# The order of 24 gate tiles beside two block inverses: sigmoid tiles first, silu tiles last

## The chip, the cores and the metric

The program runs on one core of a Trainium2 chip. The metric is the time of one launch on the device in microseconds (us). The engines of the core run side by side, each through its own instructions in order: PE (TensorE, matmuls), DVE (VectorE), ACT (ScalarE), POOL (GpSimd) and SP (SyncE, which here only issues DMAs; ACT issues some too).

## The reference

One layer of a diffusion backbone: 2048 latent and 256 context tokens of width 1024, float32. The normalized input `h` goes through one wide projection that feeds two token mixers and four gates; the mixers' outputs are gated and merged:

```python
qkv, beta_r, decay_r, kb, vb = _split_cols(h @ w_state, STATE_SIZES)
za, qb, zb, ga, gb = _split_cols(h @ w_rest, REST_SIZES)       # 512, 512, 512, 1024, 1024 columns
qa, ka, va, g, bt = _gdn_inputs(qkv, beta_r, decay_r, conv_w, a_log, dt_bias)
oa, _, _ = _gdn_bidir(qa, ka, va, g, bt, s_f, s_b, True)       # mixer A, a scan over 64-token chunks
ya = _rmsnorm(oa, gdn_norm_w) * silu(za)
ob = _latent_attention(qb, kb, vb, kb_c, vb_c, sink)           # mixer B, windowed attention
yb = ob * silu(zb)
y = sigmoid(ga) * (ya @ w_proj_a) + sigmoid(gb) * (yb @ w_proj_b)
x = x + gate[:, None] * (y @ w_out)
```

Mixer A is a gated delta rule in chunked form. Per chunk and head it needs the inverse of a unit lower triangular 64x64 matrix (`triangular_solve` in the reference). `gate` is a third of `silu(c) @ w_mod + b_mod`.

## The kernel before, in words

**Stages.** The input projection for q, k, v; then the gates of token blocks 2 and 3 beside two batches of block inverses (about 629 to 910 us of the profiled execution, the stretch that the change edits); then the scan of mixer A, beside which the gates of token blocks 1 and 0 run as fill; attention; the rest of the gates; projections and output.

**A gate tile.** The gates' 3072 columns are cut in 24 feature tiles of 128, numbered `m`: 0 to 3 are `za`, 4 to 7 `zb` (both under silu), 8 to 15 `ga`, 16 to 23 `gb` (both under sigmoid). Tokens are cut in four blocks of 512 (`gi`). `gates(ms, gis, ...)` goes through the tiles in the order of the list `ms`, and for each through the token blocks of `gis`; it asks for the next tile's weights after the first block of a tile (`rest`, L804; `gates`, L830). `beside` is another piece of work, here the gate third of `w_mod` (`mod_gate`, L212), of which one bit is written down per tile.

**Weights.** float32 products are made of three matmuls of halves. `weights` (L235) loads a tile in two pieces (`wr`, L241, on SP's queue, two buffers), rounds each to its high half `wh` (L243 on ACT in this stretch, L245 on POOL for other callers), and has DVE subtract to get the low half `wl` (L246). `wh` and `wl` have two buffers each. `fm_dense` (L521) multiplies: for each of 8 slices of 128 rows one matmul wh x hh (L524), one wh x hl (L525), one wl x hh (L526): 24 matmuls, 128x128 by 128x512, into one of three PSUM buffers (`rps`).

**What follows the matmuls** is in `rest_run` (L811): ACT takes tanh of half the sum out of PSUM into `rt` (L816, two buffers). For a silu tile DVE then reads PSUM again and makes (tanh + 1) * sum (L818). A store sends `rt` to DRAM (L819): silu tiles on SP's queue, sigmoid tiles on ACT's:

```python
        S.activation(t, ps, AF.Tanh, scale=0.5)
        if m < 8:
            V.scalar_tensor_tensor(t, t, 1.0, ps, op0=ALU.add, op1=ALU.mult)
        (dma if m < 8 else adma)(dst[gi][mm], t)
```

**The inverses.** `base` (L720) inverts 128 matrices at a time, one per partition, and is called twice. It loads `nb` and `N` (L733, L734, on SP's queue, up to 1 MB each), scales the rows of the lower and the upper half by `nb` (L737, L739, four instructions each), then makes 62 steps of a multiply (L747) and an add (L749), both on DVE, 62 to 992 elements wide; POOL clears the upper triangles (L754), a store sends the result to `Xsp` (L759). `base4` (L764) does the four remaining chunks during the scan (L784 and on).

**mod_gate** loads `w_mod` rows (L220, SP's queue), scales them on ACT (L221), adds them up on POOL (L223), sums over partitions with one matmul (L227), adds the bias on DVE (L230, L231) and stores.

**The scan** loads its operands on SP's queue (L1002, L1004, L1083, L1085 and others), merges inverses of 64 tokens to 128 (L1011 to L1034: TensorE `mtp`, `myp`, `mep`; DVE L1019, L1025) and then goes through a chain per step: `ksps` (L1093), DVE L1095, `vps` (L1099), DVE L1102, `sps` (L1111), the state S on DVE (L1114 at first, L1117 later). The memory of its first loads is that of the blocks `hh` and `hl` of the gates before, so these loads wait for the last matmul of the first gates.

**What sets the order.** A list scheduler puts the instructions of the whole program on each engine in an order of its own when the program is built; what is written in the kernel gives the dependences and a rank. On the chip that order is fixed: an engine runs its instructions one by one, and one that waits holds up all behind it.

Of the kernel before, what the change touches and what calls it, by code (L numbers as in the profile page):

```python
# [32 lines left out]
def hybrid(tc, ins, out, dbg=None, upto=9):  # L33
    nc = tc.nc
    V, S, G, T = nc.vector, nc.scalar, nc.gpsimd, nc.tensor
    ctx = ExitStack()
    with ctx:
        _hybrid(ctx, tc, nc, V, S, G, T, ins, out, dbg, upto)


def _hybrid(ctx, tc, nc, V, S, G, T, ins, out, dbg, upto):
# [103 lines left out]
    def psum(tag, shape, dt=F32, name=None):  # L145
        _, p, banks = pst["left" if tag in pst["left"][2] else "right"]
        return p.tile(shape, dt, name=name or tag, tag=tag, bufs=banks[tag])
# [64 lines left out]
    def mod_gate(pool, ones):  # L212


        for n in range(2):
            cs_ = slice(2 * D + n * 512, 2 * D + n * 512 + 512)
            gacc = pool.tile([128, 512], F32, name="gacc", bufs=1)
            for k in range(KT):
                wm = pool.tile([128, 512], F32, name="wmg", bufs=2)
                dma(wm, ins["w_mod"][0, k * 128:(k + 1) * 128, cs_])  # L220
                S.activation(wm if k else gacc, wm, AF.Copy, scale=silc[:, k, 0:1])  # L221
                if k:
                    G.tensor_tensor(gacc, gacc, wm, op=ALU.add)  # L223
                yield
            yield
            gsum = psum(f"gd{n}", [1, 512], name=f"gsum{n}")
            T.matmul(gsum, lhsT=ones[:, 0:1], rhs=gacc, start=True, stop=True)  # L227
            grow = ev.tile([1, 512], F32, name="grow", tag="rt")
            dma(grow, ins["b_mod"][:, cs_])
            V.tensor_tensor(grow, gsum, grow, op=ALU.add)  # L230
            V.tensor_scalar(grow, grow, 0.5, None, op0=ALU.mult)  # L231
            dma(gsp[:, n * 512:n * 512 + 512], grow)
            yield
# [274 lines left out]
    le, ge, gt, lt, ones = (mats[:, j] for j in range(5))  # L508
# [295 lines left out]
    def rest(ev, m, by_act):  # L804

        col, dst, mm = ((C_ZA, zasp, m) if m < 4 else (C_ZB, zbsp, m - 4) if m < 8 else
                        (C_GA, gasp, m - 8) if m < 16 else (C_GB, gbsp, m - 16))
        w = weights(w_in[:, col + mm * 128:col + mm * 128 + 128], KT, by_act)
        return w, dst, mm

    def rest_run(ev, job, m, gi):  # L811
        w, dst, mm = job
        ps = acc([128, 512], name="rps")
        fm_dense(ps, w, hh[gi], hl[gi])
        t = ev.tile([128, 512], F32, name="rt", bufs=2)
# [4 lines that stand above are left out]
# [10 lines left out]
    def gates(ms, gis, beside=(), by_act=False):  # L830
        beside = iter(beside)
        job = rest(ev, ms[0], by_act)
        for i, m in enumerate(ms):
            for j, gi in enumerate(gis):
                rest_run(ev, job, m, gi)
                if j == 0:
                    nxt = rest(ev, ms[i + 1], by_act) if i + 1 < len(ms) else None
                    next(beside, None)
            job = nxt
# [1 line left out]
    bs2_ = tc.tile_pool(name="base2", bufs=1, reuse_waits="tile")  # L841
    bs2 = bs2_.__enter__()
    with tc.tile_pool(name="gate", bufs=1, reuse_waits="tile") as gp:
        gates(list(range(24)), (2, 3), mod_gate(gp, ones), by_act=True)
    LAST = (LAT(14, 15), LAT(0, 1))
    for si, (fr, bk, np_) in enumerate((([0, 1] + LAT(*range(0, 6)), [0, 1] + LAT(*range(10, 16)), bs),
                                        (LAT(*range(6, 14)), LAT(*range(2, 10)), bs2))):
# [532 lines left out]
```

## Time and profile before

| | |
|---|---|
| time, median of 3 runs | 2011.59 us (2009.54 to 2018.15) |
| the profiled execution | 2010.84 us, span 2009.1 us |
| mean granted TensorE clock | 0.988 |
| busy: PE, DVE, ACT, POOL | 96%, 70%, 39%, 33% of the span |
| busiest groups of TensorE | rps L524, L525, L526: 308.4, 306.4, 308.3 us |
| L818, DVE | 32 instructions, 664 to 690 ns each; 16 of them in the gates of blocks 2 and 3 |
| L246, DVE (all tiles) | 120 instructions of 128x512, 776 ns in the mean |

The profile is of one execution. Its times start with the first instruction of the span; an instruction is named by its line in the kernel, with what it writes and reads (`rt<-rt,rps`). An idle time is written in brackets behind the instruction that ended it, with what released that instruction. Matmuls overlap, so their listed 0.39 us is longer than the 0.23 us from one to the next; a few per cent of the matmuls are missing in the record.

### The profile page before, as it was taken

The page shows a single profiled execution, that of the slowest core. Times are in us where ns is not written, and L with a number is a line of the kernel's source. Part 1 is how long each engine was busy: PE and PEld are TensorE (multiplying, and loading weights), DVE is VectorE, ACT ScalarE, POOL GpSimd, SP SyncE. Part 2 cuts the span into 40 slices and gives each one's busy share as a digit, 9 for nine tenths or more (in the row PEclk, how much of TensorE's full clock was granted, in tenths as well). Part 3 has the DMA queues.
Part 4 walks back from the last instruction along what each step waited for, and adds up shares of the span by engine and source line. Part 5 has one row for each costly group of instructions (what it writes and reads, how often), then busy time and mean ns, then how long its engine had stood idle before and what let it go on. Part 6 is the DMA issues. An engine that isn't in the chain of part 4 may idle for free. (4 is left out here: it accounts for less than half of the span.)

```text
span 2009.1 us, 32070 instructions
## 1 busy us (share of the span) xinstructions
PE 1936.4 (96%) x11043; PEld 1625.3 (81%) x11043; DVE 1407.5 (70%) x2780; ACT 786.1 (39%) x1975; POOL 654.0 (33%) x751
## 2 busy tenths in 40 slices
PE   6999999989999999999999999999999999999999
PEld 3888888778998778877888888888778887878887
DVE  7979766667776899999777776536687878643322
ACT  5755545544443322211222233225665656531100
POOL 1752111225443212004222234323555444432221
PEclk8999999999999999999999999999999999999999
DMA  7552326764546633537887777674455555365542
GB/s 260 166 137 83 102 87 157 184 162 147 167 142 164 184 115 110 142 100 215 230 245 221 235 207 217 195 218 129 150 184 166 184 162 178 90 195 181 183 141 94
DMA packets 375511, 333.11 MB, mean 166 GB/s; under 512 B 83833, under 2 KB 299185, under 8 KB 374709
## 3 DMA queue, kind: packets, MB, share of 16 engines
q1 hardware_dynamic: 347924, 288.59, 49.7%
q10 hardware_dynamic: 27424, 42.48, 5.9%
q8 instruction: 87, 1.43, 0.3%
q14 instruction: 76, 0.61, 0.1%
HBM read 220.28 MB, written 109.13 MB: 164 GB/s over the span
## 5 line engine op out<-in xcount | busy, mean ns | idle before, releaser
L524 PE MATMUL rps<-hh,wh 128*128 128x512 f32 x768 | 308.4, 402 | 5.4 <-DVE rt L818 4.2
L526 PE MATMUL rps<-hh,wl 128*128 128x512 f32 x768 | 308.3, 402 | 0.0
L525 PE MATMUL rps<-hl,wh 128*128 128x512 f32 x768 | 306.4, 399 | 0.0
L563 DVE SCALAR_TENSOR_TENSOR cacc<-y,cw,cacc 128x512 f32<-128x512 f32 (+1 forms) x224 | 162.8, 748 | 22.4 <-ACT cacc L561 18.2
L524 PEld LDWEIGHTS rps<-hh,wh 128*128 128x128 f32 x768 | 145.0, 189 | 40.1 <-DVE rt L818 4.8
L524 PE MATMUL lps<-hh,wh 128*128 128x512 f32 (+1 forms) x448 | 171.4, 383 | 0.2 <-ACT y L634 0.2
L526 PE MATMUL lps<-hh,wl 128*128 128x512 f32 (+1 forms) x448 | 171.5, 383 | 0.0
L526 PEld LDWEIGHTS rps<-hh,wl 128*128 128x128 f32 x768 | 145.0, 189 | 32.6
L525 PE MATMUL lps<-hl,wh 128*128 128x512 f32 (+1 forms) x448 | 171.2, 382 | 0.0
L525 PEld LDWEIGHTS rps<-hl,wh 128*128 128x128 f32 x768 | 145.0, 189 | 32.4
L945 DVE TENSOR_TENSOR pl<-pt,ph 128x512 fp32r<-128x512 f32 x156 | 105.5, 686 | 42.1 <-ACT ph L943 41.2
L943 ACT CAST ph<-pt 128x512 fp32r<-128x512 f32 x156 | 90.1, 584 | 110.2 <-PE pt L941 77.2
L917 DVE CUSTOM_DVE_ANT_0 pr<-sc,band,sk 128x640 f32<-128x640 f32 (+1 forms) x128 | 106.8, 862 | 32.7 <-PE sc L913 16.9
L816 ACT ACTIVATE rt<-rps 128x512 f32<-128x512 f32 x96 | 57.2, 595 | 176.0 <-PE rps L526 159.1
L749 DVE TENSOR_TENSOR N<-N,btmp 128x62 f32<-128x62 f32 (+30 forms) x124 | 117.7, 949 | 3.0
L747 DVE TENSOR_TENSOR btmp<-N 128x62 f32<-128x62 f32 (+30 forms) x124 | 116.1, 936 | 3.1
L927 POOL TENSOR_SCALAR pr<-pr,sm 128x640 f32<-128x640 f32 (+1 forms) x128 | 99.2, 794 | 56.1 <-DVE sm L925 38.3
L1229 PE MATMUL pps<-yh,wph 128*128 128x512 f32 x256 | 105.2, 415 | 7.2 <-ACT yh L1211 5.0
L919 ACT ACTIVATE pr<-pr,sm 128x640 f32<-128x640 f32 (+1 forms) x128 | 104.0, 815 | 19.8 <-DVE sm L917 19.8
L246 DVE TENSOR_TENSOR wl<-wr,wh 128x512 fp32r<-128x512 f32 x120 | 91.6, 776 | 23.9 <-POOL wh L245 21.3
L245 POOL TENSOR_SCALAR wh<-wr 128x512 fp32r<-128x512 f32 x72 | 48.1, 683 | 167.1 <-PE lps L525 67.6
L1230 PE MATMUL pps<-yl,wph 128*128 128x512 f32 x256 | 101.7, 397 | 0.0
(301 smaller groups left out, 4922.8 us busy)
## 6 DMA issues: line engine op xcount, KB each, us to landing
wr<-in_w_in_dram SPq DMA_DIRECT2D x120, 256.0 KB
kw<-Ksp SPq DMA_DIRECT2D x28, 384.0 KB
x<-vsp SPq DMA_DIRECT2D x36, 256.0 KB
k<-ksp SPq DMA_DIRECT2D x34, 256.0 KB
kT<-kTsp SPq DMA_DIRECT2D x34, 256.0 KB
wm<-in_w_mod_dram SPq DMA_DIRECT2D x16, 512.0 KB
xt<-in_x_dram SPq DMA_DIRECT2D x16, 512.0 KB
dtl<-Dsp SPq DMA_DIRECT2D x32, 256.0 KB
```

Source lines behind the costliest of these rows:

```text
L524: T.matmul(ps, lhsT=wh[:, k], rhs=xh[:, k], start=k == 0, stop=False)
L525: T.matmul(ps, lhsT=wh[:, k], rhs=xl[:, k], start=False, stop=False)
L526: T.matmul(ps, lhsT=wl[:, k], rhs=xh[:, k], start=False, stop=k == kt - 1)
L563: V.scalar_tensor_tensor(a, y[:, t:t + n], cw[:, m, t:t + 1], a, op0=ALU.mult, op1=ALU.add)
L747: V.tensor_tensor(tv, A[:, m + 1:, m].unsqueeze(2).to_broadcast([h1 + n, r, m]), A[:, m, 0:m].unsqueeze(1).to_broadcast([h1 + n, r, m]), o ...
L749: V.tensor_tensor(A[:, m + 1:, 0:m], A[:, m + 1:, 0:m], tv, op=ALU.add)
L917: V.tensor_tensor_reduce(s_, ps[:, o:768], band[:, b0:b0 + W + 256], -0.125, sk[:, 1, hd:hd + 1], ALU.add, ALU.min, sm[:, h, 1:2])
L919: S.activation(s_, s_, AF.Exp, scale=-1.0, bias=sm[:, h, 1:2], accum_out=sm[:, h, 2:3])
L927: G.tensor_scalar(p[:, h, :W + 256], p[:, h, :W + 256], sm[:, h, 3:4], 1.0, op0=ALU.mult, op1=ALU.mult)
L945: V.tensor_tensor(pl, pt, f32(ph), op=ALU.subtract)
L1229: T.matmul(ps, lhsT=wh[:, k, ms], rhs=hs[k], start=k == 0, stop=False)
L1230: T.matmul(ps, lhsT=wh[:, k, ms], rhs=ls[k], start=False, stop=False)
```

## The change

The list of tiles of the first `gates` call is written in another order. Nothing else is edited; the later calls (`gates` at L1176, L1180 and L1251) keep theirs.

```diff
@@ -841,7 +841,7 @@
     bs2 = bs2_.__enter__()
     with tc.tile_pool(name="gate", bufs=1, reuse_waits="tile") as gp:
-        gates(list(range(24)), (2, 3), mod_gate(gp, ones), by_act=True)
+        gates(list(range(8, 24)) + list(range(8)), (2, 3), mod_gate(gp, ones), by_act=True)
     LAST = (LAT(14, 15), LAT(0, 1))
```

Since the scheduler decides, the order of the other engines' work changes too. On DVE, where the first inverse begins (L737 and L739 are its scalings, L747 its first step; - is before, + after):

```order
 L737 TENSOR_TENSOR N<-N,nb 64x1024
-L246 TENSOR_TENSOR wl<-wr,wh 128x512 x2
-L818 SCALAR_TENSOR_TENSOR rt<-rt,rps 128x512
+L246 TENSOR_TENSOR wl<-wr,wh 128x512
 L739 TENSOR_TENSOR N<-N,nb 64x16x16
 L739 TENSOR_TENSOR N<-N,nb 64x16x32
 L739 TENSOR_TENSOR N<-N,nb 64x16x48
 L739 TENSOR_TENSOR N<-N,nb 64x1024
-L818 SCALAR_TENSOR_TENSOR rt<-rt,rps 128x512
 L747 TENSOR_TENSOR btmp<-N 128x62
 L749 TENSOR_TENSOR N<-N,btmp 128x62
```

The L818 that stood before and behind the scalings of L739 are gone, and the two L246 of a tile stand apart.

On DVE in the second inverse, at the two L246 of the thirteenth tile of the list. Before:

```order
L749 TENSOR_TENSOR N<-N,btmp 128x25x38
L246 TENSOR_TENSOR wl<-wr,wh 128x512
L747 TENSOR_TENSOR btmp<-N 128x936
L246 TENSOR_TENSOR wl<-wr,wh 128x512
L749 TENSOR_TENSOR N<-N,btmp 128x24x39
```

After:

```order
L749 TENSOR_TENSOR N<-N,btmp 128x23x40
L747 TENSOR_TENSOR btmp<-N 128x902
L749 TENSOR_TENSOR N<-N,btmp 128x22x41
L246 TENSOR_TENSOR wl<-wr,wh 128x512
L747 TENSOR_TENSOR btmp<-N 128x882
L246 TENSOR_TENSOR wl<-wr,wh 128x512
L749 TENSOR_TENSOR N<-N,btmp 128x21x42
```

The pair stands four widths later: counted from the second inverse's L739, 66 instructions of L747 and L749 stand ahead of it before, and 70 after, and twelve L818 before and none after.

On SP, where the scan's first loads (L1004, L1083) begin; wr are weights. Before:

```order
L241 DMA wr<-in_w_in_dram 128x4x128 x8
L229 DMA grow<-in_b_mod_dram 1x512
L232 DMA gsp<-grow 1x512
L241 DMA wr<-in_w_in_dram 128x4x128 x8
L1004 DMA moff_10009<-offsp_91 64x256
L1004 DMA moff_10015<-offsp_92 64x256
L1083 DMA k_10055<-ksp 128x512
```

After:

```order
L819 DMA zbsp_124<-rt 128x512
L819 DMA zbsp_123<-rt 128x512
L241 DMA wr<-in_w_in_dram 128x4x128
L819 DMA zbsp_124<-rt 128x512
L241 DMA wr<-in_w_in_dram 128x4x128
L819 DMA zbsp_123<-rt 128x512
L1004 DMA moff_10009<-offsp_91 64x256
L1004 DMA moff_10015<-offsp_92 64x256
L1083 DMA k_10055<-ksp 128x512
```

The last silu stores (L819) now stand between the weight loads, and one stands straight ahead of the scan's first load. The very last one comes about 24 loads later. The 16 stores of sigmoid tiles that are first in the list are issued by ACT, each behind its tanh.

## Rows read from the trace of the kernel before

**Rows 1.** The page, part 1: busy time, share of the span, instructions.
```profile
PE   6999999989999999999999999999999999999999
```

**Rows 2.** Waits of TensorE, 600 to 1350: us in total, times, longest.
```profile
PE rps L524 <- DVE rt L818: 4.2, 1, 4.2
...
PE ksps L1093 <- DVE S L1117: 2.9, 1, 2.9
...
PE mep L1028 <- DVE moff L1025: 1.8, 1, 1.8
```

**Rows 3.** A window: each engine's busy us, granted clock (PEclk), DMA share, GB/s.
```profile
672.00:680.00 8.00, 4.35 (x10) 3.47 (x11) 7.93 (x11) 4.53 (x7) 4.22 (x4) 0.63 0.49 146
```

**Rows 4.** Timeline, TensorE: start, us, instruction, [idle before, and for what].
```profile
671.06 0.39 PE L526 MATMUL rps<-hh,wl 128*128 128x512 f32 x1
...
675.65 0.79 PE L524 MATMUL rps<-hh,wh 128*128 128x512 f32 x1 [4.20 <-DVE rt L818]
...
683.73 0.40 PE L524 MATMUL rps<-hh,wh 128*128 128x512 f32 x1
...
689.33 0.40 PE L524 MATMUL rps<-hh,wh 128*128 128x512 f32 x1
...
694.93 0.40 PE L524 MATMUL rps<-hh,wh 128*128 128x512 f32 x1
```

**Rows 5.** Timeline, VectorE, 671 to 677.
```profile
671.84 3.04 DVE L739 TENSOR_TENSOR N<-N,nb 64x256 f32<-64x256 f32 x4 [2.34 <-DMA N<-Nsp]
...
674.91 0.69 DVE L818 SCALAR_TENSOR_TENSOR rt<-rt,rps 128x512 f32<-128x512 f32 x1
...
675.51 0.87 DVE L747 TENSOR_TENSOR btmp<-N 128x342 f32<-128x342 f32 x1
...
676.42 1.47 DVE L749 TENSOR_TENSOR N<-N,btmp 128x342 f32<-128x342 f32 x1
```

**Rows 6.** Timeline, SyncE's queue and Scalar, 659 to 675.
```profile
659.94 0.33 SPq L819 DMA_DIRECT2D zasp<-rt  x1
...
662.63 0.59 ACT L816 ACTIVATE rt<-rps 128x512 f32<-128x512 f32 x1
...
672.14 0.60 ACT L816 ACTIVATE rt<-rps 128x512 f32<-128x512 f32 x1 [8.92 <-DMA zasp<-rt]
...
674.21 1.30 ACT L243 CAST wh<-wr 128x512 fp32r<-128x512 f32 x2
```

**Rows 7.** Timeline, VectorE: low halves of the weights of places 5 and 12.
```profile
691.40 0.69 DVE L246 TENSOR_TENSOR wl<-wr,wh 128x512 fp32r<-128x512 f32 x1
...
772.18 0.68 DVE L246 TENSOR_TENSOR wl<-wr,wh 128x512 fp32r<-128x512 f32 x1
```

**Rows 8.** VectorE's timeline, and POOL's groups in 744 to 772 (busy us, mean ns).
```profile
747.62 2.17 DVE L749 TENSOR_TENSOR N<-N,btmp 128x992 f32<-128x992 f32 x1
...
751.53 1.17 DVE L749 TENSOR_TENSOR N<-N,btmp 128x990 f32<-128x990 f32 x1
...
L223 POOL TENSOR_TENSOR gacc<-gacc,wmg 128x512 f32<-128x512 f32 x7 | 14.1, 2010 | 12.3 <-ACT wmg L221 9.7 <-ACT gacc L221 2.5
```

**Rows 9.** VectorE: a window, and the group of L246 in 690 to 919.
```profile
810.00:919.00 109.00, 109.00 (x466) 86.78 (x465) 102.31 (x127) 18.75 (x33) 9.91 (x12) 1.00 0.44 123
...
L246 DVE TENSOR_TENSOR wl<-wr,wh 128x512 fp32r<-128x512 f32 x42 | 30.1, 730 | 3.9 <-ACT wh L243 2.0 <-POOL wh L245 1.9
```

**Rows 10.** Timelines at the scan's start: SyncE's queue, VectorE, TensorE.
```profile
910.22 1.12 SPq L1004 DMA_DIRECT2D moff<-offsp  x2
...
938.38 0.68 DVE L1102 TENSOR_TENSOR v<-vps,brs 128x512 f32<-128x512 f32 x1
...
939.12 1.16 PE L1111 MATMUL sps<-v,k 128*128 128x128 f32 x8 [1.29 <-DVE v L1102]
```

**Rows 11.** A window of the scan, columns as in rows 3.
```profile
1262.00:1270.00 8.00, 5.11 (x35) 4.45 (x34) 6.31 (x15) 1.98 (x9) 5.66 (x8) 1.00 0.81 243
```

## The prediction

> **What bounds the kernel now.** I read the page's busy shares first. TensorE is busy for 96% of the span [rows 1], so nothing that only relieves VectorE or a queue changes the end; what counts is where TensorE waits or runs slowly. The list of TensorE's waits is therefore the second view, cut to 600 to 1350 us, the stretch whose instructions the change moves. It has one large wait in the gate stage, 4.2 us for the step L818 of VectorE, and two in the scan, 2.9 and 1.8 us [rows 2]. The third view is the clock by windows: in 672 to 680 us TensorE was granted 0.63 of full speed, so it spent most of that window at the lower of its levels (1.2 and not 2.4 GHz), right behind that wait [rows 3]. The fourth is TensorE's timeline. I call the 24 matmuls of one feature tile on one block of tokens a pass (passes 0 to 47), and a tile's position in the list its place (places 0 to 23, two passes each). Pass 6 issues its last matmul at 671.06 and, at 0.23 us a matmul, is through at 671.29. Pass 7 starts at 675.65, pass 8 at 683.73, pass 9 at 689.33, pass 10 at 694.93 [rows 4]. So the wait is 675.65 - 671.29 = 4.36 us; pass 7 lasts 8.08 where pass 8 or 9 lasts 5.60, another 2.48. One event costs 6.84 us.
>
> Why does it wait? A pass needs one of three PSUM buffers, and pass 7 gets that of pass 4. Pass 4 is a silu tile, and its buffer is read last by L818 at 674.91 on VectorE, in order behind the L739 multiplies of the second inverse, which began at 671.84 after 2.34 us of waiting for N to land [rows 5]. Scalar has its own delay: its tanh of pass 4 starts only at 672.14, after 8.92 us of waiting for the store of pass 2, issued on SyncE at 659.94 [rows 6]; that store was late because its L818 too had stood behind an L739 waiting for N. The two inverses' loads thus reach TensorE only through L818.
>
> **The change part by part.** It adds and removes no arithmetic. Sixteen L818 leave the passes 0 to 15 and return in passes 32 to 47; sixteen stores leave SyncE's queue where N, the weights and w_mod are loaded, and their data goes on Scalar's queue; the same number comes back to SyncE late.
>
> *The wait at 671 goes.* Place 2 is then a sigmoid tile, whose tanh is the last reader of PSUM. The store of pass 2 is issued by Scalar itself right behind its tanh, near 650 instead of 659.94. Even if it takes as long to land as before (659.94 to 672.14, 12.2 us) it is there at 662.4. The tanh of pass 3 ran at 662.63 [rows 6], that of pass 4 can follow at 663.3, eight us before TensorE asks at 671.29. Pass 5's buffer is asked for at 676.9. Its tanh stands behind the same w_mod scalings and casts that ended with the cast at 674.21 (1.30 us) [rows 6], so it ends by 676.1. I take the whole 6.84 as removed: 0 to 6.84.
>
> *What is late next: the low halves of the weights.* VectorE computes them (wl, L246) between the steps of the inverses, and TensorE, 6.84 us earlier, asks for them earlier. VectorE cannot start the second inverse earlier, because that start is the landing of N (671.84).
> For place 5, wl began at 691.40 [rows 7]. From L739 on, three L818 are gone in front of it (674.91 is one; 0.60 us from one start to the next, 674.91 to 675.51 [rows 5]): -1.80. The two instructions of width 342, which took 0.87 and 1.47 [rows 5], now run before L739, in time that VectorE waited anyhow: -2.34 as timed, or -0.80 at the rate of the undisturbed 990-wide one, 1.17 us [rows 8], if the slowing falls on their successors. Three wider ones (612 to 650) are put in front: 3 x 0.77 = +2.3 at the same rate, an estimate. Together -0.3 to -1.84. With its 0.69, wl is ready at 690.25 to 691.8. TensorE uses it in the third matmul of the pass, 0.47 after the start, so place 5 starts at 689.8 to 691.3, against 694.93: 3.6 to 5.1 of the 6.84 are kept.
> For place 12, wl began at 772.18 [rows 7], and the place started near 683.73 + 16 x 5.60 = 773.3. Twelve L818 are gone: -7.2. But the list now has 70 inverse instructions ahead of it instead of 66, all near their widest. At 1.17 each that is +4.7; at the 2.17 of a slow one [rows 8], +8.7. So wl is ready between 770.4 and 774.4, which keeps at most 3.4 us or loses 0.6. I take 1.17: in 744 to 772 POOL ran eight instructions (seven L223 [rows 8] and one more) and seven of VectorE's were slow, so the slow ones are as many as POOL's, not a share of VectorE's. This is the narrowest place by my count; 3.4 us stay.
>
> The Trainium skill, "SBUF — State Buffer", section "SBUF: two separate sides", has a rule on this: a GpSimd instruction and a VectorE instruction with two SBUF inputs exclude each other for one whole instruction. The count of slow instructions agrees. By the rule, place 12 keeps 3.4, as taken; by a slowing of every instruction in the stretch it would lose 0.6 and the time would be 2011.4. The rule also speaks against the change: L818 reads PSUM and one SBUF operand, so beside it POOL could run freely, and without it POOL's 4.22 us in 672 to 680 [rows 3] falls on blockable work. By it place 5 loses up to 1.80 x 4.22 / 8 = 0.95 more and keeps 2.65, for a time of 2008.2.
>
> *The returning L818.* VectorE was busy 102.31 of 109 us in 810 to 919 [rows 9], so 6.7 us are free, and sixteen L818 want 16 x 0.60 = 9.6. What covers the rest is that VectorE has run ahead: its list puts four to fifteen more inverse instructions before the low halves of places 12 to 16. It can use that only if it does not wait for the weights' high halves; before, such waits came to 3.9 us in 690 to 919 [rows 9]. From the second inverse's L739 to the first L1102 there are now 18 L818 instead of 14 (+2.4), three inverse instructions fewer, two of them the 342-wide (-0.8 at the plain rate) and one 572-wide (-0.7): +0.9, and the waits shrink by up to 3.9 as TensorE frees weights earlier. The bounds of the first L1102 (938.38, for which TensorE waited 1.29 us at 939.12 [rows 10]) are then -3.0 and +0.9. I take -3.0, as the last wait before it is itself for a cast that TensorE's progress releases. That leaves the 1.29 wait about 0.4 longer.
>
> *SyncE's queue at the tail.* The last silu stores now stand ahead of the scan's first loads (issued 910.22 on the last matmul of the gates [rows 10]). They need their L818 by then; my count has the last but one near 903, so 0, and one for one beyond 910. What is queued behind them is every load of the first scan step.
>
> *The later scan.* The list puts up to 21 more fill matmuls (4.9 us) ahead of the same scan instruction, which leaves the last four finalizing steps less to hide under. At most the waits of 2.9, 1.8 and 1.3 there go (-6.0); at worst four steps wait like the worst now, 4 x 2.9 = +11.6. Nothing orders these, so 0.
>
> Sum: -6.84 + 3.44 handed back + 0.4 + 0 = -3.0. The profiled execution took 2010.84 us (span 2009.1), so 2007.8 is predicted; the median of three runs, 2011.59, lies 0.75 above the profiled one, within their spread.
>
> **The rivals.**
> A is the forecast: the wait goes, half is handed back at wl, 2007.8 (2003 to 2013, from place 5's upper bound 5.1 with one scan wait of 2.9 gone, to 0.6 lost at place 12 with the scan 1.5 worse).
> B, all is kept: VectorE's slowing by POOL lands elsewhere and wl is never late: 2010.84 - 6.84 = 2004.0; if the scan's three waits go as well, 1998.0. For it: wl of place 5 misses by little. Against: VectorE is nearly full from 690 on.
> C, slower: VectorE's time freed in the early places is lost in waits for high halves, so the 9.6 us of returning L818 meet only 6.7 free ones. It then reaches L1102 2.9 us later than before; TensorE waits 1.29 + 2.9 = 4.2 there, all its lead turns into waiting, and the clock falls as it did behind the 4.36 us wait, 2.48 more: 2010.84 + 2.9 + 2.48 = 2016.2. It decides from the point where VectorE is not at least 2.9 us ahead at 810. Against the clock part: in 1262 to 1270, with a 2.9 us wait, the clock stayed at 1.00 [rows 11]. For it: VectorE is the fullest there is beside TensorE.
> D, the change doesn't do what it says: the buffer at 671 is held by Scalar, not by L818, because its in-order stream still stands behind w_mod loads or its own stores: 2010.8. For it: the 8.92 us. Against: that wait's cause was the store's late issue.
>
> **How the numbers follow.** A 0.52, B 0.17, C 0.15, D 0.12; 0.04 is left for the scan's last steps going badly alone. A change within 0.5%, 10 us, can hardly be told from none in measuring this kernel. Faster than 2001.5 needs B with the scan's waits: 0.09. Slower than 2021.6 needs C plus part of the 11.6, or the latter on its own: 0.07. The rest is 0.84. The range for 8 in 10 takes in A, D, C's 2016.2 and most of B: 2001 to 2017.
>
> **What would show it.** The wait of rps for L818 near 671 is absent and no window in 664 to 690 shows a clock under 1.00 (if it is still there, D). TensorE has new short waits for wl L246 at places 4, 5, 11 to 13, together 3 to 4 us (none: B). The first L1102 starts near 935.4 (later than 938.4: C). The waits at ksps and mep keep their 2.9 and 1.8. The prediction fails if TensorE's waits between 690 and 940 exceed 7 us, or if the scan's last four steps gain waits that I put at nothing.

## The result: slower by 0.2%, and the profile after

The changed kernel takes 2016.99 us in the median of 20 runs (2011.05 to 2019.07), the kernel before 2011.93 of 20 (2006.91 to 2018.15). The ratio of the means is 1.0021, with an interval from 1.0013 to 1.0029. That is 4.2 us slower, where 3.0 faster was predicted. The median lies inside the range of 2001 to 2017, and the difference is under the 0.5% that the forecast called hard to tell from none; but the sign is wrong, and by more than the measurement leaves open. The profiled execution of the changed kernel took 2013.37 us (span 2011.6).

In [rows 1] the line shown is that of the forty slices; the 96% stands in the table above it. After, TensorE's line in the page's first part (busy us, share of the span, instructions) is nearly what it was, 1936.4 us before:

```profile
PE 1938.4 (96%) x11043; PEld 1626.8 (81%) x11043; DVE 1406.6 (70%) x2780; ACT 787.8 (39%) x1975; POOL 657.2 (33%) x751
```

The largest waits of TensorE in 600 to 1350 us, which answer to [rows 2]:

```profile
PE rps L526 <- DVE wl L246: 3.1, 3, 1.9
PE mtp L1013 <- POOL mx L998: 2.5, 1, 2.5
PE rps L524 <- POOL wh L245: 2.0, 1, 2.0
PE aps L1135 <- DVE oa L1147: 1.7, 2, 0.9
```

The 4.2 us for L818 are gone, and so are the 2.9 at ksps and the 1.8 at mep. Waits for wl, for the high halves wh and for mx stand in their place.

TensorE's timeline of the gates after, to be read against [rows 4]:

```profile
671.49 0.39 PE L524 MATMUL rps<-hh,wh 128*128 128x512 f32 x1
...
679.69 0.50 PE L526 MATMUL rps<-hh,wl 128*128 128x512 f32 x1 [1.88 <-DVE wl L246]
...
693.45 0.50 PE L526 MATMUL rps<-hh,wl 128*128 128x512 f32 x1 [0.75 <-DVE wl L246]
...
774.04 0.50 PE L526 MATMUL rps<-hh,wl 128*128 128x512 f32 x1 [0.45 <-DVE wl L246]
```

Pass 7 starts without a wait. Then places 4, 5 and 12 wait for their low halves. The same on VectorE, with columns as in [rows 5]; these answer to [rows 5, 7, 10]:

```profile
672.18 3.04 DVE L739 TENSOR_TENSOR N<-N,nb 64x256 f32<-64x256 f32 x4 [1.30 <-DMA N<-Nsp]
675.26 1.55 DVE L747 TENSOR_TENSOR btmp<-N 128x392 f32<-128x392 f32 x1
676.84 1.54 DVE L749 TENSOR_TENSOR N<-N,btmp 128x392 f32<-128x392 f32 x1
...
678.96 1.29 DVE L246 TENSOR_TENSOR wl<-wr,wh 128x512 fp32r<-128x512 f32 x2
...
692.72 0.68 DVE L246 TENSOR_TENSOR wl<-wr,wh 128x512 fp32r<-128x512 f32 x1
...
826.76 1.35 DVE L246 TENSOR_TENSOR wl<-wr,wh 128x512 fp32r<-128x512 f32 x2 [2.80 <-ACT wh L243]
...
938.70 0.68 DVE L1102 TENSOR_TENSOR v<-vps,brs 128x512 f32<-128x512 f32 x1
```

The first L1102 (the step that the scan's first `sps` waits for) starts at 938.70 against 938.38 before: no lead at all on VectorE.

Windows of the changed kernel, with columns as in [rows 3] (busy time of PE, PEld, DVE, ACT and POOL, each with its count; the granted clock is the third figure from the end):

```profile
672.00:680.00 8.00, 6.12 (x26) 4.50 (x25) 7.71 (x9) 3.91 (x6) 3.86 (x3) 1.00 0.57 185
680.00:688.00 8.00, 8.00 (x29) 6.36 (x28) 7.79 (x8) 3.82 (x7) 4.87 (x4) 0.79 0.64 203
...
940.00:945.00 5.00, 5.00 (x21) 4.18 (x20) 4.91 (x8) 0.60 (x1) 3.59 (x4) 0.69 0.68 174
...
1274.00:1280.00 6.00, 4.60 (x28) 3.98 (x29) 3.17 (x8) 2.46 (x10) 1.78 (x6) 0.51 0.39 93
1280.00:1286.00 6.00, 6.00 (x18) 4.66 (x18) 0.69 (x1) 0.00 (x0) 2.50 (x4) 0.63 0.64 150
```

The clock is full in 672 to 680, where it was 0.63. It falls to 0.79 a little later, behind the wait at place 4, to 0.69 at the scan's start, and to 0.51 and 0.63 at 1274 to 1286. That last fall is new; [rows 11] had 1.00 behind a wait of 2.89. Two waits of TensorE stand ahead of it (timeline after):

```profile
939.48 0.66 PE L524 MATMUL rps<-hh,wh 128*128 128x512 f32 x1 [2.00 <-POOL wh L245]
...
1274.47 0.69 PE L1013 MATMUL mtp<-ident,mx 64*128 64x64 f32 x4 [2.46 <-POOL mx L998]
...
1276.08 2.08 PE L1135 MATMUL aps<-S,qT 128*128 128x128 f32 x8 [0.93 <-DVE oa L1147]
```

**Where the time went.** I cut the span at two instructions of TensorE: the first merge of inverses (L1011) and the first of attention (L910). Within a stage, idle is the time TensorE is not busy, and the clock's loss is TensorE's busy time times (1 - granted clock), both summed over windows of 4 us (the first begins at a whole multiple of 4 us, at most 3 us behind the L1011). One execution is too little for this: four more kernels below (e4, e9, e10, e16) have the order of one of the two on all compute engines, but for three rows of VectorE in e16, and both kernels were profiled again, so that there are five executions of each order. In us:

| order | gates | scan | rest | first 100 us of the scan: idle, clock's loss | from 320 us of the scan on: idle, clock's loss |
|---|---|---|---|---|---|
| before | 290.9 | 431.9 | 657.6 | 3.2, 0.0 | 4.2, 0.0 |
| before, again (e5) | 290.7 | 436.5 | 657.1 | 3.0, 1.7 | 5.2, 2.7 |
| before, again (e6) | 290.8 | 431.5 | 653.6 | 2.8, 0.0 | 4.5, 0.0 |
| before's order (e4) | 289.2 | 437.9 | 658.4 | 3.1, 3.2 | 4.7, 2.7 |
| before's order (e10) | 288.6 | 433.3 | 657.1 | 2.5, 0.0 | 5.4, 1.4 |
| **mean** | **290.0** | **434.2** | **656.8** | **2.9, 1.0** | **4.8, 1.4** |
| changed | 289.2 | 439.5 | 654.0 | 3.0, 1.6 | 5.5, 4.3 |
| changed, again (e7) | 289.6 | 441.2 | 654.1 | 5.0, 0.0 | 5.0, 4.4 |
| changed, again (e8) | 289.8 | 441.1 | 657.4 | 6.3, 0.0 | 5.6, 3.1 |
| changed order (e9) | 289.4 | 442.0 | 655.2 | 4.3, 1.2 | 4.5, 4.6 |
| changed order (e16) | 289.5 | 441.4 | 654.5 | 4.3, 3.2 | 5.3, 3.4 |
| **mean** | **289.5** | **441.0** | **655.0** | **4.6, 1.2** | **5.2, 4.0** |

The gates gain 0.5, the scan loses 6.8, the rest gains 1.7: 4.6 in all, which fits the 4.2 of the ratio. The rest runs in the same order in both kernels and takes 653.6 to 658.4 us in the executions of before's order alone, so its 1.7 says little. Three fill matmuls (0.7 us) have moved from ahead of the first L1011 to behind it, so the gates' own gain is nil, and 0.7 of the scan's loss is work. Of the remaining 6.1, 1.7 are idle time at the scan's start and 2.6 the lower clock in the last steps; 0.4, 0.2 and 0.1 are idle and clock elsewhere. (The 1.7 depends on the cut: at exactly 100 us behind the L1011 it is 1.2, and 0.6 then lie in the middle.) About 1.1 I could not place. e16 has a wait of its own at the scan's start (experiment 4); without it the scan's mean is 441.0, and the clock's loss at the start 0.7 instead of 1.2.

### The profile page after: what moved, and what is told of

It is laid out like the page before. It is cut to its first block, busy times and chain, and to the rows that moved or that the text cites. A ratio compares the mean times of both kernels' runs of the same rounds, so it can differ in the third digit from the quotient of the medians.

```text
span 2011.6 us, 32060 instructions
## 1 busy us (share of the span) xinstructions
PE 1938.4 (96%) x11043; PEld 1626.8 (81%) x11043; DVE 1406.6 (70%) x2780; ACT 787.8 (39%) x1975; POOL 657.2 (33%) x751
## 5 line engine op out<-in xcount | busy, mean ns | idle before, releaser
L749 DVE TENSOR_TENSOR N<-N,btmp 128x62 f32<-128x62 f32 (+30 forms) x124 | 117.0, 943 | 3.1
L747 DVE TENSOR_TENSOR btmp<-N 128x62 f32<-128x62 f32 (+30 forms) x124 | 115.1, 928 | 3.1
L246 DVE TENSOR_TENSOR wl<-wr,wh 128x512 fp32r<-128x512 f32 x120 | 92.4, 787 | 32.0 <-POOL wh L245 23.6
L1231 PE MATMUL pps<-yh,wpl 128*128 128x512 f32 x256 | 101.5, 396 | 0.0
```

Of the source, the lines that this page charges most:

```text
L747: V.tensor_tensor(tv, A[:, m + 1:, m].unsqueeze(2).to_broadcast([h1 + n, r, m]), A[:, m, 0:m].unsqueeze(1).to_broadcast([h1 + n, r, m]), o ...
L749: V.tensor_tensor(A[:, m + 1:, 0:m], A[:, m + 1:, 0:m], tv, op=ALU.add)
L1231: T.matmul(ps, lhsT=wl[:, k, ms], rhs=hs[k], start=False, stop=k == 3)
```

## The experiments

**1. Is it the silu stores on SyncE, or L818 near the scan, or the order itself?** e1 keeps the list and moves the stores of blocks 2 and 3 to Scalar's queue. The scheduler then gives the scan almost the fill of the kernel before: at every eighth sps the number of fill matmuls ahead of it is within 2 of before, where the changed kernel has 5 at the first, 21 to 29 in the middle and 8 at the last more. e2 and e3 move only four tiles. e4 has the list of before, with the stores moved.

```diff
 e1, e4:  - (dma if m < 8 else adma)(dst[gi][mm], t)
          + (dma if m < 8 and gi < 2 else adma)(dst[gi][mm], t)
 e2:      + gates(list(range(8, 12)) + list(range(8)) + list(range(12, 24)), (2, 3), ...)
 e3:      + gates(list(range(4, 24)) + list(range(4)), (2, 3), ...)
```

e1:

> The changed list (16 sigmoid tiles first), but the stores of the silu tiles of blocks 2 and 3 are issued by Scalar instead of SyncE. With that the scheduler's order in the scan falls back close to that of the kernel before (TensorE differs from it in 106 rows, the changed kernel in 437; POOL in 4 against 91), while the gates keep the changed order. Theory S (the loss sits in the scan that was planned anew: in the changed kernel's trace from the scan's first merge to attention +7.6 us, in the gates -1.7): the scan costs within 2 us of before, the gates stay 1 to 3 us shorter, in all 1 to 4 us faster than before (2008 to 2011 against 2012). Rival T (the sixteen L818 that now run beside the end of the second inverse and the scan's start make the loss, wherever the rest stands): 3 to 6 us slower than before, as the change. Rival Q (the silu stores on SyncE's queue between the weight loads make the loss): as S in time, but then the order of the scan does not matter, which e3 tells.

e2:

> Only four sigmoid tiles are put ahead of the eight silu tiles (tiles 8 to 11, then 0 to 7, then 12 to 23). Scan order close to that of before (TensorE 106 rows, POOL 4). Theory S: no wait for L818 near 671 (6.8 us with its clock), some waits for the weights' low halves instead; scan within 2 us of before; 1 to 6 us faster than before (2006 to 2011). Rival T: no L818 stands at the tail, so the whole gain shows too, 2006 to 2009. If it is as slow as the change (2015 and more), neither holds and the loss lies in the gates.

e3:

> Only the four za tiles are put last (tiles 4 to 23, then 0 to 3): the list begins with silu tiles zb, so the wait near 671 can come back, and eight L818 and eight silu stores are at the tail instead of sixteen. The scan's order is that of the changed kernel (TensorE differs from it in 15 rows, POOL in 2). Theory S: the scan costs 5 to 9 us more than before, as in the change; with the wait near 671 back, 2014 to 2020. Rival T and Q: half the tail, so half the loss, and 2012 to 2016 with the wait back.

e4:

> The kernel before, with the sixteen silu stores of blocks 2 and 3 issued by Scalar instead of SyncE; the orders of TensorE, VectorE and POOL are unchanged to the row. Theory S and T: the wait for L818 near 671 stays within 1.5 us, as N's landing sets it; same as before within 2 us. Rival Q: faster, 2 to 5 us, as the loads on SyncE's queue are freed of the stores.

Ratios to before: e1 1.0025 (1.001 to 1.0039), e2 1.0033 (1.0018 to 1.0048), e3 1.0021 (1.0006 to 1.0036), e4 0.9997 (0.9982 to 1.0012). Theory S, by which e1 and e2 gain, fails in both. The stores' queue is not it (e4), nor is it L818 at the end of the list alone: e2 has none there, and its scan takes 441.4 us, with a wait of 4.3 at mep. Not all of e2's loss is in the scan, though: its gates take 294.8, with waits of 0.9, 0.8 and 1.8 for L818 left in them. e3, with half of the L818 at the end, has the wait near 671 back at 2.1, gates of 287.4 and a scan of 438.3. The fill brought forward is not it by itself either: e1 lacks that and loses as much, at other places. TensorE's largest waits in e1, 600 to 1350:

```profile
PE rps L526 <- DVE wl L246: 4.1, 3, 2.2
PE ksps L1093 <- DVE S L1117: 4.0, 1, 4.0
PE mep L1028 <- DVE moff L1025: 3.8, 1, 3.8
PE sps L1111 <- DVE v L1102: 1.9, 1, 1.9
```

The waits at sps, mep and ksps are those of before ([rows 2, 10]: 1.3, 1.8, 2.9). At sps and mep e1 waits longer than any of the five executions of before's order (1.2 to 1.7 and 1.1 to 1.8); its 4.0 at ksps is within theirs (1.6 to 4.1). The changed kernel has others in their place.

**2. How much is chance?** e5 and e6 are the kernel before, e7 and e8 the changed one, unchanged, one profiled execution each.

e5:

> The kernel before, unchanged, profiled again. Theory K (chance of the clock): the profile that the prediction was read from is an execution without a fall of TensorE's clock in the scan, and others of the same kernel have some (e4, whose TensorE, VectorE and POOL orders are those of before, lost 5.9 us of TensorE's time to a lower clock in the scan behind waits of 1.7, 1.4 and 3.5 us); so here 0 to 6 us are lost in the scan. Theory V (VectorE's longer way through the second inverse): the waits of TensorE keep their lengths, near 671 4 us, sps 1.3, mep 1.8, ksps 2.9, each within 1 us.

e6:

> As e5, once more: theory K wants a different clock loss in the scan from one execution to the next with the same waits; theory V wants the last instruction of the second inverse (L749, 62 wide) within 1.5 us of 966.5.

e7:

> The changed kernel, unchanged, profiled again. Theory S: the waits for POOL's high halves near 939 (2.0 us) and for POOL's mx near 1274 (2.5 us) come again, each with a clock fall, 5 to 6 us lost to the clock in the scan. Theory K: the loss in the scan is anywhere in 0 to 6. Theory V: the last instruction of the second inverse 2 to 4 us later than in the kernel before.

e8:

> As e7, once more. If the sum of TensorE's waits and clock losses between 629 us and attention is larger than in the kernel before by 4 to 6 us in each of the three executions, the loss is in this stretch and not in the later stages, whose orders are the same in both kernels.

They took 2018.47, 2003.46, 2016.0 and 2017.54 us. In e5 the wait at ksps was longer, and the clock fell behind it (timeline of TensorE, then a window):

```profile
1270.13 2.07 PE L1093 MATMUL ksps<-S,kT 128*128 128x128 f32 x8 [4.05 <-DVE S L1117]
```
```profile
1268.00:1272.00 4.00, 1.87 (x9) 1.87 (x9) 3.42 (x8) 1.18 (x5) 2.24 (x4) 0.68 0.76 191
```

In e6 that wait was 1.58, and the scan lost nothing to the clock. So before's clock in the last steps is a matter of the execution: its loss is 0.0, 2.7, 0.0, 2.7 and 1.4 in the table. With the changed order it is between 3.1 and 4.6 in all five. The two waits near 1275 return in e7 and e8. TensorE's timeline in e7, and a window behind:

```profile
1277.19 0.61 PE L1013 MATMUL mtp<-ident,mx 64*128 64x64 f32 x4 [2.25 <-POOL mx L998]
...
1278.81 2.07 PE L1135 MATMUL aps<-S,qT 128*128 128x128 f32 x8 [1.00 <-DVE oa L1147]
```
```profile
1280.00:1286.00 6.00, 6.00 (x29) 4.79 (x28) 2.14 (x6) 1.37 (x6) 3.65 (x7) 0.50 0.60 152
```

**3. The last steps.** Ahead of the wait for mx, POOL stood for 11.39 us before x, a load that SyncE issued at 1262.28, in a row of issues with hardly a gap in which the loads of x4 (L997) stand too. Timelines of the changed kernel, POOL and then SyncE's queue:

```profile
1267.18 1.04 POOL L1086 TENSOR_TENSOR x<-x,rin 128x512 f32<-128x512 f32 x1 [11.39 <-DMA x<-vsp]
...
1272.78 1.64 POOL L998 COPY mx<-x 64x256 f32<-64x256 f32 x2
```
```profile
1262.28 0.93 SPq L1085 DMA_DIRECT2D x<-vsp  x2
```

e11 and e12 move the 32 loads of x4 to Scalar's queue, in the changed kernel and in that before. e9 and e10 move the stores of the second inverse's result instead, on the theory that the last inverse was late through them.

```diff
 e11, e12: - dma(x4[bs_, q], X4sp[...])
           + adma(x4[bs_, q], X4sp[...])
 e9, e10:  - dma(Xset[d][si]..., N[p0:p0 + n]...)                   (L759)
           + (adma if si else dma)(Xset[d][si]..., N[p0:p0 + n]...)
```

e9:

> The changed kernel; only the two stores of the second inverse (L759, Xsp) are issued by Scalar instead of SyncE; orders of TensorE, VectorE and POOL the same to the row. Theory L (the last inverse starts late: in the changed kernel its first multiply L784 begins 365 to 366.5 us after the gates' first matmul, before 358.6 to 359.1, because these stores, and so the loads of N behind them, come late on SyncE's queue; the scan's last merges then miss their operands near 1274): L784 begins 2 to 4 us sooner, and the kernel is 1 to 4 us faster than the change (2012 to 2015). Rival F (the fill matmuls were planned out of the scan's last steps, so that any lateness there shows): L784 may move, the wait for mx near 1274 stays within 0.7 us of 2.4, and the time stays as the change's, 2015 to 2018.

e10:

> The kernel before with the same two stores issued by Scalar; orders of the other engines the same to the row. Theories L and F: nothing was late here, same as before within 2 us, 2010 to 2014.

e11:

> The changed kernel; the 32 small loads of the last inverse's result (L997, x4) are issued by Scalar instead of SyncE, whose queue issues without a pause from 1251 to 1264. The list moves a little (TensorE 308 rows, all in the scan's last steps). Theory W (near 1274 TensorE waits because SyncE's queue is the limit: POOL waits 11.4 us for an x issued at 1262): the wait for mx goes below 1 us, no clock fall there, 3 to 6 us faster than the change, 2010 to 2013. Rival F: the last steps wait for VectorE or POOL instead, together 3 us or more between 1255 and 1345 and still a clock fall; 2014 to 2018.

e12:

> The kernel before with the same 32 loads on Scalar's queue (TensorE 265 rows of difference). Theory W: the wait of ksps near 1265 (1.6 to 4.0 us in four executions, the longest two with a clock fall) goes too, 2 to 5 us faster than before: 2007 to 2010. Rival F: same as before within 2 us.

Ratios: e9 1.0032 (1.0019 to 1.0046), e10 0.9992 (0.9978 to 1.0006), e11 0.9988 (0.9975 to 1.0), e12 0.9989 (0.9978 to 0.9999). e9 refutes its theory: the last inverse (first L784) is no earlier, 364.9 us after the first gate matmul against 365.0 in the changed kernel and 359.1 before. With e11 the loss is gone: the changed list is then as fast as before's list with the same edit, and both a little faster than the kernel before. In e11 TensorE has no wait for mx and the clock holds (its largest waits in 600 to 1350, then a window):

```profile
PE rps L526 <- DVE wl L246: 3.9, 2, 3.4
PE rps L524 <- ACT rt L816: 3.2, 5, 1.1
PE ops L1146 <- DVE oa L1143: 1.7, 1, 1.7
```
```profile
1274.00:1280.00 6.00, 5.40 (x42) 4.19 (x41) 4.67 (x10) 1.61 (x8) 2.29 (x6) 1.00 0.66 184
```

But the reason that I gave, SyncE's queue, is not what e11 shows. POOL's timeline in e11:

```profile
1268.62 1.04 POOL L1086 TENSOR_TENSOR x<-x,rin 128x512 f32<-128x512 f32 x1 [7.49 <-DMA x<-vsp]
...
1275.16 1.33 POOL L998 COPY mx<-x 64x256 f32<-64x256 f32 x2 [1.19 <-DMA x<-X4sp]
```

POOL waits for x here too, and mx is written later than in the changed kernel, 1275.16 against 1272.78 (0.6 later if counted from the gates' first matmul). What differs is TensorE's order: with these loads elsewhere the scheduler laid out the last steps anew and held back 48 of the 922 fill matmuls of the scan for later (24 of 919 in e12). That is why the scan of e11 is 424.4 us and the rest 665.6. So the experiment shows that the loss can be had back by moving these loads, which changes the queue and the layout of the last steps at once. That it is the layout is likely, since mx comes no earlier, but not shown.

**4. The scan's start.** e13 joins the edits of e1 and e11, so the scan has before's fill but in the last steps; e14 does so with before's list. e15 adds to e13, and e16 to the changed kernel alone, the loads of N for the last inverse (L777) and the stores of L759 on Scalar's queue, to have that inverse start earlier.

```diff
 e15, e16: - dma(N[p0:p0 + 16], Nsp[d][c:c + 2]...)                 (L777)
           + adma(N[p0:p0 + 16], Nsp[d][c:c + 2]...)
```

e13:

> The changed list with both sets of DMAs on Scalar: the sixteen silu stores (as e1) and the 32 x4 loads (as e11). The order of the scan is then that of e12 but for its first steps (TensorE 106 rows, POOL 4), so that e13 against e12 is the list alone. Theory W (the whole loss of the change was the scan's end on SyncE's queue): same as e12 within 2 us, 2007 to 2012. Rival E (the scan's start loses too: in e1 TensorE waited 3.8 us at mep, behind L784, and 1.9 at sps, before 1.8 and 1.3, with a clock fall of 2 us): 2 to 4 us slower than e12, 2011 to 2014, with mep waiting over 3 us.

e14:

> The kernel before with both sets of DMAs on Scalar (e4 and e12 together); TensorE, VectorE and POOL as in e12 to the row. If the two gains add, 0.9986 of before, 2008 to 2010; theory Q (the stores on SyncE's queue matter) has held nothing so far, so I expect no difference from e12 within 2 us.

e15:

> The changed list with the silu stores of blocks 2 and 3 and the x4 loads on Scalar's queue, and now the last inverse's loads of N (L777) and the stores of the second inverse's result (L759) on Scalar too. TensorE's order differs from that of the kernel with the stores and x4 loads on Scalar only in some rows of the scan. Theory N (what costs at the scan's start is that N of the last inverse lands late, because its load stands on SyncE behind slow issues, 984.96 to a first L784 at 994.30): the first L784 starts by 991, the waits at sps, mep and ops, 2.8, 3.2 and 2.9 us, lose at least half of their sum, and the ratio to before goes from 1.001 to about 0.9988. Rival E2 (VectorE is late at the scan's start by the sixteen silu steps alone, N has slack): L784 may be sooner, but sps and mep wait as long and the ratio stays between 1.000 and 1.002.

e16:

> The changed list with only the last inverse's loads of N (L777) and the second inverse's stores (L759) on Scalar's queue; the compute engines' orders are those of the changed kernel but for three rows of VectorE. Theory W (the loss is in the last steps, where SyncE's x4 loads hold up POOL's L1086 and so the wait of mtp for mx; N only made the planner put fill there): L784 starts earlier than 993.9, by 991, and still the wait near 1274 and the fall of the clock behind it remain, ratio 1.001 to 1.003. Rival N: with N in time the scan loses nothing, ratio 0.9975 to 0.9995 and a scan stage of about 433 us and not 440.

Ratios: e13 1.001 (0.9996 to 1.0024), e14 0.9988 (0.9975 to 1.0001; its profiled execution took 3793.32 us and is left out, so it has times alone), e15 1.0017 (1.0001 to 1.0033), e16 1.0021 (1.0004 to 1.0039). e13 and e14 differ in the list only: 2009.9 and 2006.29 us on the same chip, beside 2008.96 for before. The last steps of e13 are quiet (idle 2.1, no loss to the clock), and most of its loss stands at the start: 6.0 us idle and 5.8 lost to the clock in the first 100 us. The wait at ops is later, at 1164, with another 1.4 lost to the clock. Three of TensorE's waits in e13, and two windows:

```profile
PE mep L1028 <- DVE moff L1025: 3.2, 1, 3.2
PE ops L1146 <- DVE oa L1140: 2.9, 1, 2.9
PE sps L1111 <- DVE v L1102: 2.8, 1, 2.8
```
```profile
936.00:944.00 8.00, 5.19 (x27) 4.02 (x26) 7.84 (x13) 1.67 (x3) 3.82 (x6) 0.72 0.83 239
996.00:1004.00 8.00, 5.44 (x30) 4.84 (x31) 8.00 (x16) 0.76 (x2) 1.33 (x3) 0.59 1.02 307
```

VectorE is full there, 7.84 and 8.00 of 8 us, and TensorE waits for it. But in 936 to 944 it was as full before (7.90, and 7.87 in e12), so that is no mark of the changed list. In 996 to 1004 it was not (6.17, and 6.70 in e12): there the last inverse begins, at 994.3 in e13 and at 988.5 in e12. e15 and e16 failed to do what they were for: the loads went out on Scalar no sooner, and L784 started 364 and 365 us after the first gate matmul, as late as ever. Nor were they free: Scalar stood behind these loads, and in e16 TensorE then waited 1.63 us for Scalar's L1107 at 988.44, with a fall of the clock, as in no other execution of the changed order. e16, Scalar with its queue, and VectorE:

```profile
984.78 1.19 ACTq L777 DMA_DIRECT2D N<-Nsp  x2
986.07 0.60 ACT L816 ACTIVATE rt<-rps 128x512 f32<-128x512 f32 x1 [10.45 <-DMA mx<-Xsp]
```
```profile
994.92 3.02 DVE L784 TENSOR_TENSOR N<-N,btmp 32x256 f32<-32x256 f32 x4 [0.94 <-DMA N<-Nsp]
```

So whether the late N costs anything stays untested. In e15 the three waits shown for e13 came to 4.2 us and not 8.9, as theory N asked, but L784 was no earlier, new waits of 1.0 for Scalar's L1107 came, and no time was gained, so this does not bear the theory out. In e16 the wait for mx (2.1 us) and the fall of the clock came again, as the theory of the last steps expected.

**The list alone.** Five pairs differ in the list of tiles and in what the scheduler makes of it. The changed list's mean time, as a share of the other's, is 1.0021 (the change), 1.0028 (e1 to e4), 1.0041 (e9 to e10), 1.0022 (e13 to e14) and 0.9995 (e11 to e12). So the list costs time in four of the pairs, and nothing where only the loads of x4 were moved.

## Why the prediction was wrong, step by step

Three groups of rows that the list rests on. Places 4 and 5, TensorE in e7:

```profile
680.72 0.50 PE L526 MATMUL rps<-hh,wl 128*128 128x512 f32 x1 [2.02 <-DVE wl L246]
...
694.37 0.50 PE L526 MATMUL rps<-hh,wl 128*128 128x512 f32 x1 [2.18 <-DVE wl L246]
```

Place 12, TensorE before, then VectorE after:

```profile
745.42 1.02 PE L227 MATMUL gsum<-gacc,mats 128*1 128x512 f32 x2
...
774.94 0.40 PE L526 MATMUL rps<-hh,wl 128*128 128x512 f32 x1
```
```profile
773.30 0.69 DVE L246 TENSOR_TENSOR wl<-wr,wh 128x512 fp32r<-128x512 f32 x1
```

The scan's start, TensorE in e8:

```profile
938.33 0.47 PE L524 MATMUL rps<-hh,wh 128*128 128x512 f32 x1 [1.68 <-DVE rt L818]
```

- **The wait at 671 goes: right.** Pass 7 follows pass 6 without a gap, and the clock stays full there; rival D is out. In the five executions of before's order this wait is 2.4 to 5.0 us, so the 4.2 was no extreme.
- **wl is late next: right in kind, and the first step that failed, in its size.** I counted 3.44 of the 6.84 handed back; nearly all was. I left out place 4, which has a pair of L246 behind two 392-wide steps of 1.55 and 1.54 us: TensorE waited 1.88 there, and the clock fell to 0.79 in 680 to 688. That fall cost nothing. In e7, e8 and e16 the clock holds, TensorE instead waits 2.2 at place 5 and not 0.75 (the rows of e7), and the gates take 289.5 to 289.8 us against 289.2 and 289.4 with the fall. What counts is when VectorE has wl. Place 5's began at 692.72, where I had 689.6 to 691.1: of the 6.84, place 5 kept 1.95 (its third matmul at 693.45, before at 694.93 + 0.47), not 3.6 to 5.1. Place 12 kept 0.90 (its third matmul at 774.04, before at 774.94), not 3.4.
  The 773.3 that I had for the start of place 12 leaves out the two L227 on the way; it was 774.48. On VectorE the way from the first L739 to this wl took 101.12 us (672.18 to 773.30) instead of 100.35 (671.84 to 772.18), where the sum had 2.5 less. Counted from one start to the next, the twelve L818 gave 7.2, as forecast, but the steps cost 6.9 more, not 4.7, and the L246 1.1 more, for which I had no term. The 70 steps are not the 66 and four wide ones: two of 342 fall out in front, and six of 902 to 936 come in. The scan's first load, which waits for the last of the gates' matmuls, went out at 909.42 against 910.22 [rows 10], with the gates begun 0.2 later: 1.0 gained, not 3.4, in that pair, and nothing in the mean over the five.
- **VectorE's lead at the first L1102: the next step that failed.** I took -3.0 of bounds from -3.0 to +0.9. From L739 to L1102 VectorE took 266.54 us before (671.84 to 938.38) and 266.52 after (0.4 more in the mean over the five). Counted as above, the L818 cost 2.4 more, as forecast, and the steps 3.0 less (forecast -1.5). But the waits for high halves fell only from 3.9 to 2.8, all in one at 826.76, where I had them gone, and the L246 came to 1.4 more and the others to 0.3 more, without a term. So TensorE had nothing to gain at the scan's start. Its wait of 1.29 at sps became one of 2.00 for wh, a cast of POOL that stood 2.98 us before the load of these weights and began at 938.81 (938.77 before). In e8, the same order, the wait there is 1.68 for an L818, and in e3 2.30: the step that was moved out of TensorE's way at 671 stands in it again.

  Rival C had this outcome, no lead, but not the way to it: the waits for high halves shrank and L1102 came no later than before. That the median, 2016.99, lies near C's 2016.2 is luck.
- **The later scan: the step that decides the sign.** "Nothing orders these, so 0" was wrong: it is 6.8 us (6.1 without the three matmuls), inside the bounds that I gave (-6.0 to +11.6) but far from 0. The scan's plan comes out of the same scheduler as the gates, and the changed list moves it: where the fill goes forward (the changed kernel) the largest part of the loss is in the last steps, which have 8 fill matmuls less; where it is kept (e1, e13) the loss is largely at the start. I had seen the fill moved by 21 matmuls and put a term with bounds 17.6 us apart at 0. The sign of failing that I had named came true: the last steps gained the waits for mx and oa.
- **The clock.** My price for a wait in the scan had no fall of the clock, since [rows 11] showed none behind 2.9 us. Other executions of before's order show one behind the same wait where it is longer (3.5 to 4.1 us), the changed order has one there every time, and in the last steps it is the largest single term (2.6 of 6.8).
- **SyncE's tail: right at 0.** The last silu store ahead of the scan's loads was issued at 906.59, 2.8 us ahead of the first load.

The Trainium skill, "SBUF — State Buffer", section "SBUF: two separate sides", was cited for a loss of up to 0.95 more at place 5. The trace agrees in direction: POOL was busy 3.86 + 4.87 us in 672 to 688, the 392-wide steps took 1.55 and 1.54 there (the 440-wide one behind them 0.62), and place 5 was later than by the plain rate. But the size came out larger: of the 6.84 place 5 kept 1.95, where the sum by the rule had 2.65.

**What stays open.** Why the changed order makes the scan's first 100 us idle 1.2 to 1.7 longer is not shown: VectorE is full in parts of it, but not only with the changed list, and no run moved the weights that POOL waits for at 938.81. L784 starts 6 us later, and the trace has a path for half of that. The second inverse's last upper triangle is cleared by POOL (L754), which stands behind two L1086 that wait for x, in the changed kernel:

```profile
966.43 2.04 POOL L1086 TENSOR_TENSOR x<-x,rin 128x512 f32<-128x512 f32 x2 [2.39 <-DMA x<-vsp]
968.42 0.50 POOL L754 TENSOR_SCALAR_AFFINE_SELECT N<-N 128x256 f32<-128x256 f32 x1
```

Before, L754 began at 965.47, with VectorE done at the same time (965.40 and 965.61). In e1 and e13 that path is gone, L754 follows VectorE's last step at once; but there this step itself ends 2.1 and 3.7 us later than before, counted from the gates' first matmul, and L784 is late all the same. No run has the changed list with L784 in time, and none separates the layout of the last steps from the queue that feeds them. So the scan's loss is narrowed down to places; its cause stays open.

## What to carry to other kernels

A wait that is taken from the bounding engine early is worth only what the next engine in order leaves of it; here VectorE took as long from one landmark to the next as before. Ask that first, step by step, with the instructions that really stand in the way. When one scheduler lays out several stages, an edit in one is priced in the stages behind it too, above all in those that live on shared fill; a term with bounds of -6 and +12 isn't 0, and it should have set the chances. A single profile doesn't price short waits: take several of each kernel, since the clock behind the same wait differs from one to the next.

## What the runs showed of the hardware that was not expected

Whether the granted clock falls behind a wait of TensorE is not told by the wait's length alone. At place 4, in the same order, it fell behind waits of 1.88 (the changed kernel) and 1.90 (e9), and stayed at 1.00 behind 2.02, 1.90 and 1.93 (e7, e8, e16). At ksps, in before's order, it stayed behind 1.58 (e6) and 2.89 (before) and fell behind 3.52 (e4), 3.76 (e10) and 4.05 (e5). Behind the pair of 2.46 and 0.93 it fell to 0.51, and behind such a pair it fell in all five executions of the changed order.

A fall costs time only where nothing later takes it back. In the last steps it costs 1.4 to 4.6 us, from under half of the waits ahead of it (e10) to more than these (e9). At place 4 it cost nothing, since TensorE came to wait less at place 5. The same kernel took 2003.46 us in e6 and 2018.47 in e5; 5.0 of these 15.0 lie in the scan, 3.5 behind it, and 5.5 ahead of the gates.
